# A decoder trunk on one core: K and Q blocks by seven products, a delta rule with fewer VectorE operations, and joint turns in the MLP

## The chip, the cores and the metric

The kernel runs on one core of a Trainium2 chip. The metric is the device time of one execution in microseconds (us). The engines are named as in the profile: PE (matmuls, and PEld for its weight loads), DVE (VectorE), ACT (ScalarE), POOL (GpSimd) and SP (SyncE, which here only issues DMAs). Each engine runs its own instructions in order; they wait for one another through semaphores.

## What is computed

One layer of a hybrid decoder trunk for 256 tokens of width 2048, in float32. Cut to what matters here:

```
h = rmsnorm(x)
q, k, v, z, b, a, p_in, g_a, g_b = split(h @ w_in)
q, k, v = silu(causal_dwconv(q | k | v))               # width 4
o   = gated_delta_rule(l2norm(q) * 128**-0.5, l2norm(k), v, g_log, beta)   # 16 heads of 128
y_a = rmsnorm(o) * silu(z)
y_b = einsum(pooled(p_in), pool_w) * pool_scale        # four groups of 512
x  += (sigmoid(g_a) * y_a + sigmoid(g_b) * y_b) @ w_out
gate, up = split(rmsnorm(x) @ w_up)                    # 2 x 5632
x  += (gelu(causal_dwconv(gate) + b) * up) @ w_down
return rmsnorm(x)
```

The delta rule needs, per head and chunk of tokens, decays exp(g_i - g_j) for i >= j and the solution of a unit lower triangular system.

## The kernel before

**A weight tile.** All large products read their weights from HBM as tiles of 256 rows (a feature block) by 512 columns. Each float32 value is used as a high and a low part. A tile goes through four steps: SP starts a DMA into `raw` (4 buffers); ACT copies it into `whi` (L317, 3 buffers), which rounds it; DVE subtracts to get `wlo` (L328, 3 buffers; this is called the split below); PE does 12 matmuls of 128x512: two halves `kk` of the block, two halves `t` of the tokens, and three products (high x high L365, low x high L366, high x low L367). `srcs` lists the tiles in the order in which they are used, and `weights()` returns the next one after it has started cast and split up to two tiles ahead. With three buffers the cast of tile n waits until PE has left tile n-3.

**Groups.** The input projection runs in four groups of four heads. Group g reads, eight tiles each, K, Q, V, the pooled input, the gate GB, then Z and the pool product, and the gate GA. A result is two PSUM banks, [128, 2, 512], from the pool `psm` (2 buffers); small results use `psg` (4 buffers).

**Side work.** The delta rule of group g is the generator `gdn()`, advanced by one step after each half tile (`side()`), so that its instructions lie between the matmuls of its group and of the next. It makes decays (L879 on DVE, L888 on ACT), Gram matrices (`ga`), inverts the triangular matrix's diagonal blocks of 32x32 on DVE (`B0` = 32; L965 and L967, into `tb`, which holds eight columns of a block in a partition), sends them through DRAM (`tbd`) to `TT`, and doubles the size of the inverse in steps on PE: L1011, L1029, L1039, L1047, L1054 with results taken by ACT (`U`) or DVE (L987, L1022, L1031, L1032, L1048). What is left is drained behind GA; `gated` (L1211, L1215) multiplies by the gate and adds the pooled part. Around it L1204 and L1206 apply GA and the norm weight to `sz`. Callables in `later` run behind the first tile of the next result.

**Order.** Within each engine the order comes from a scheduler which simulates a timeline over the program as it is written; from the end of group four on PE's order is fixed as written. `issue_after` adds an order between two instructions.

**Seven products.** In the MLP, pairs of feature blocks of the up projection are multiplied as 2x2 blocks (tokens in halves by features in halves, times features in halves by gate and up) with seven block products instead of eight, called T1, 11, T2, 21, T3, 22, T4. T1 to T4 use sums of weight blocks that DVE forms in `quad` tiles (L244, 128x1024), and token sums (`ups`) formed once; L1433 and similar sum partial results in PSUM. A product is 6 matmuls of 128x512 (L1418): it takes half the tokens of a tile. The results of gate and up are turned from token rows to feature rows by eight PE transposes each (L1480).

## Time and profile before

| | |
|---|---|
| three runs | 1536.61, 1536.89, 1537.75 us, median 1536.89 |
| profiled execution | span 1536.8 us |
| SP, weights of the input projection | 224 DMAs of 512 KB, 4.3 us from issue to landing |
| ACT casts of `raw`, L317 | 420, mean 1052 ns |
| DVE weight sums, L244 | 72, mean 1216 ns |

The profiled execution has no time of its own beside its span of 1536.8 us, and it is held against the median of the runs. A row of a group reads: line, engine, operation, what is written <- what is read, shape, count | busy us, mean ns | idle time of the engine just before, and what ended it. A row of a timeline reads: start, duration, engine, line, operation, in brackets the idle time before it and its releaser. Matmul records overlap, so their pitch is read from start to start. In the slices each digit is a fortieth of the span. A row of waits gives the engine, what it waited for, us in total, times and the longest.

### The profile page before, as it was taken

To read this page: it belongs to the slowest core of one execution; us is meant where nothing else is said; L and a number is where in the kernel's file an instruction comes from. 1 tells how busy PE (TensorE), PEld (TensorE's weight loads), DVE (VectorE), ACT (ScalarE), POOL (GpSimd) and SP (SyncE) were. 2 spreads that over 40 slices of the span, in tenths; PEclk is the share of its full clock that TensorE was granted. 3 is DMA by queue.
4 is the path that set the end of the run, shared out by engine and by line. 5 is a ranking of instruction groups with operands and counts; after the bars stand their busy time and mean duration, and the time that the engine had idled before them with its cause. 6 is when DMAs were issued, how large, how long until landed. Compare 5 with 4: busy or idle time off the path is not lost. (4 is left out here: it accounts for less than half of the span.)

```text
span 1536.8 us, 20233 instructions
## 1 busy us (share of the span) xinstructions
PE 1524.3 (99%) x7290; PEld 1255.4 (82%) x7290; DVE 1268.3 (83%) x1793; ACT 853.1 (56%) x1070; POOL 80.9 (5%) x105
## 2 busy tenths in 40 slices
PE   9999999999999999999999999999999999999997
PEld 8887888787878888788888888788888888888876
DVE  6788859896589858887567899999999886889896
ACT  6455446454455445454455666666666665555553
POOL 1010002000100000000000000000000011010200
PEclk9999999999999999999999999999999999999999
DMA  8776757776576766776588556656457478566662
GB/s 276 209 229 198 203 165 207 218 216 185 148 250 201 208 169 194 231 195 186 171 263 305 179 178 219 219 206 206 154 165 243 127 238 266 172 223 207 235 201 98
DMA packets 166515, 313.62 MB, mean 204 GB/s; under 512 B 19554, under 2 KB 23426, under 8 KB 166286
## 3 DMA queue, kind: packets, MB, share of 16 engines
q1 hardware_dynamic: 157280, 283.17, 59.2%
q0 software_dynamic: 7344, 27.27, 5.5%
q10 hardware_dynamic: 1790, 1.89, 0.4%
q8 instruction: 57, 0.93, 0.3%
q14 instruction: 44, 0.36, 0.1%
HBM read 303.33 MB, written 8.95 MB: 203 GB/s over the span
## 5 line engine op out<-in xcount | busy, mean ns | idle before, releaser
L317 ACT CAST whi<-raw 128x1024 fp32r<-128x1024 f32 x420 | 441.2, 1052 | 427.1 <-PE psm L366 270.0
L328 DVE TENSOR_TENSOR wlo<-raw,whi 128x1024 fp32r<-128x1024 f32 x418 | 507.7, 1220 | 146.0 <-ACT whi L317 140.2
L317 ACT CAST whi<-quad 128x1024 fp32r<-128x1024 f32 x182 | 190.5, 1053 | 136.8 <-PE psg L1418 43.5
L328 DVE TENSOR_TENSOR wlo<-quad,whi 128x1024 fp32r<-128x1024 f32 x182 | 220.0, 1219 | 30.0 <-ACT whi L317 29.4
L367 PE MATMUL psm<-wlo,xhl 128*128 128x512 f32 x432 | 169.5, 393 | 1.3 <-DVE wlo L328 1.2
L365 PE MATMUL psm<-whi,xhl 128*128 128x512 f32 x432 | 169.0, 391 | 0.0
L366 PE MATMUL psm<-whi,xhl 128*128 128x512 f32 x432 | 168.6, 390 | 0.0
L1418 PE MATMUL psg<-whi,fhl 128*128 128x512 f32 x504 | 127.2, 390 | 0.0
L1418 PEld LDWEIGHTS psg<-whi,fhl 128*128 128x128 f32 x504 | 94.5, 188 | 19.6
L367 PEld LDWEIGHTS psm<-wlo,xhl 128*128 128x128 f32 x432 | 81.1, 188 | 18.8 <-DVE wlo L328 2.2
L366 PEld LDWEIGHTS psm<-whi,xhl 128*128 128x128 f32 x432 | 81.1, 188 | 16.8
L365 PEld LDWEIGHTS psm<-whi,xhl 128*128 128x128 f32 x432 | 81.1, 188 | 16.7
L244 DVE TENSOR_TENSOR quad<-quad,quad 128x1024 f32<-128x1024 f32 x72 | 87.6, 1216 | 0.0
L1418 PE MATMUL psg<-wlo,fhl 128*128 128x512 f32 x252 | 69.9, 389 | 0.0
L1418 PE MATMUL psg<-whi,ups 128*128 128x512 f32 x216 | 58.9, 394 | 0.0
L1418 PEld LDWEIGHTS psg<-wlo,fhl 128*128 128x128 f32 x252 | 47.3, 188 | 9.9
L1403 PE MATMUL psm<-whi,hhi 128*128 128x512 f32 (+1 forms) x140 | 54.5, 389 | 0.1
L1403 PE MATMUL psm<-whi,hlo 128*128 128x512 f32 (+1 forms) x140 | 54.1, 386 | 0.0
L1403 PE MATMUL psm<-wlo,hhi 128*128 128x512 f32 (+1 forms) x140 | 54.0, 387 | 0.0
L365 PE MATMUL psm<-whi,mhi 128*128 128x512 f32 x128 | 50.8, 397 | 0.0
L367 PE MATMUL psm<-wlo,mhi 128*128 128x512 f32 x128 | 50.0, 390 | 0.0
L366 PE MATMUL psm<-whi,mlo 128*128 128x512 f32 x128 | 49.9, 390 | 0.0
(435 smaller groups left out, 2953.7 us busy)
## 6 DMA issues: line engine op xcount, KB each, us to landing
raw<-in_w_in_dram SPq DMA_DIRECT2D x224, 512.0 KB, 4.3
raw<-in_w_up_dram SPq DMA_DIRECT2D x104, 512.0 KB, 4.8
quad<-in_w_up_dram SPq DMA_DIRECT2D x72, 512.0 KB, 5.0
raw<-in_w_down_dram SPq DMA_DIRECT2D x56, 512.0 KB, 5.1
raw<-in_w_out_dram SPq DMA_DIRECT2D x32, 512.0 KB, 4.2
quad<-in_w_down_dram POOLq DMA_DIRECT2D x32, 512.0 KB, 5.3
mv<-vrow SPq DMA_DIRECT2D x12, 512.0 KB, 4.8
taps<-in_conv_qkv_w_dram SPq DMA_DIRECT2D x16, 256.0 KB, 6.6
```

The source lines that it names most:

```text
L244: nc.vector.tensor_tensor(out_, plus_, minus_, op=ALU.subtract)
L317: last_cast[0] = nc.scalar.copy(hi, raw).ins
L328: last_split[0] = nc.vector.tensor_tensor(lo, raw, hi.bitcast(F32), op=ALU.subtract).ins
L365: mm(ps[:, t, :], lh(k, t), hi[:, kk, :], start=(k == 0), stop=False)
L366: mm(ps[:, t, :], ll(k, t), hi[:, kk, :], start=False, stop=False)
L367: mm(ps[:, t, :], lh(k, t), lo[:, kk, :], start=False, stop=(k == nk - 1))
L1403: mm(ps[:, cs], lhs(kk), part_[:, kk, cs], start=(first and kk == 0 and n == 0), stop=(last and kk == 1 and n == 2), skip_group_check=shared)
L1418: mm(ps, lhs(kk), w[n][:, kk], start=(first and n == 0 and kk == 0 and lhs is high), stop=False, skip_group_check=True)
```

## The change

Three parts are changed at once.

1. In groups two to four, the first four feature blocks (tiles 0 and 1 of 256 rows) of K and of Q are computed together as a pair with seven products. K and Q play the parts of gate and up in the MLP. T1 and 11 stand between the last tiles of the GA gate of the group before (`KQ_FIRST`), the others between K's tiles (`KQ_THEN`); Q begins with its tile 2. DVE forms T1 to T4 (L266 in the changed kernel) and two PSUM sums (L406 and L415), ACT makes two copies. The token sums `xsums` are made once, in group one. Four tiles are loaded into `quad` buffers instead of `raw`.
2. In the delta rule the differences of running sums are not formed on DVE: POOL sets the excluded entries of the row to -1e30 and ACT takes exp with the negative sum as bias, one head and half at a time. The second half of `ga0` is scaled on ACT. The columns of a block are dealt to the partitions in turn, so that step j of the inversion works on only the first j // 4 + 1 of a partition's eight columns; `tb` and `tbd` are laid out for that. `gated` of groups one to three scales on ACT and uses two 128x1024 operations on DVE.
3. In the MLP, the gate and up results of a chunk are turned together behind the third pair of products instead of apart.

Lines of the changed kernel differ: L365 to L367 are now L390 to L392, L328 is L350, L244 is L266, L987 is L1039, L1011 to L1054 are L1063 to L1106, L1204 and L1206 are L1301 and L1303, L1418 is L423, L1480 is L1568.

```diff
+    UP_PARTS = ("T1", "11", "T2", "21", "T3", "22", "T4")
+    KQ_FIRST = (5, "11", 6, "T1", 7)
+    KQ_THEN = ("T2", "21", "T3", 2, "22", 3, "T4", 4, 5, 6, 7)
+    up_w = {("kq", g): [cols(w_in[0], base + 512 * g, KD) for base in (C_K, C_Q)] for g in range(1, 4)}
...
+            if g and base == C_K:
+                srcs += [("up", ("kq", g), step, 0) if isinstance(step, str) else tiles[step] for step in KQ_THEN]
+            else:
+                srcs += tiles[2:] if g and base == C_Q else tiles
...
+        srcs += tiles[: 5 if g < 3 else 8]
+        if g < 3:
+            srcs += [("up", ("kq", g + 1), step, 0) if isinstance(step, str) else tiles[step] for step in KQ_FIRST]
...
-            up_steps += p21 + [("gate", c)] + t3 + p22 + [("up", c)] + t4
+            up_steps += p21 + t3 + p22 + [("turns", c)] + t4
...
+    quads_behind = {}
+    for g in range(1, 4):
+        sums_behind[first_part(("kq", g)) - 1] = [(("kq", g), "T1", 0)]
+        for i in range(4):
+            quads_behind[first_part(("kq", g), "11") - 6 + i] = [(("kq", g), i)]
...
+    def pair_product(bank, what, tokens, sums):
+        a, b = bank["ps"]
+        if what in ("11", "21", "T4"):
+            j, t = {"11": (0, 0), "21": (1, 0), "T4": (1, 1)}[what]
+            high, low = (lambda kk, f=f: f(2 * j + kk, t) for f in tokens)
+        else:
+            n = {"T1": 0, "T2": 1, "T3": 2, "22": 3}[what]
+            high, low = (lambda kk, s=s: s[:, n, kk * P : (kk + 1) * P] for s in sums)
+        if what == "21":
+            nc.vector.tensor_tensor(b[:, 0], a[:, 1], bank["own"], op=ALU.add)
+        w = weights()
+        ps = {"T1": a[:, 0], "21": a[:, 0], "22": b and b[:, 0]}.get(what, a[:, 1])
+        high_first([(ps, high, low)], w, what in ("T1", "11"))
+        if what == "T1":
+            bank["own"] = cpool.tile([P, 512], F32, tag="sqj", name=nm("own"))
+            nc.scalar.copy(bank["own"], a[:, 0])
+            nc.scalar.copy(a[:, 0], a[:, 1])
+        elif what == "T3":
+            nc.vector.tensor_tensor(b[:, 1], a[:, 1], bank["own"], op=ALU.add)
...
-                                pattern=[[-1, 8], [1, B0]], compare_op=ALU.is_equal, fill=0.0, base=-8 * cq,
+                                pattern=[[-4, 8], [1, B0]], compare_op=ALU.is_equal, fill=0.0, base=-cq,
...
-        nc.vector.tensor_copy(cumc, pcc)
+        nc.vector.tensor_scalar(ncum, pcc, -1.0, None, op0=ALU.mult)
...
-        def differences(hp):
-            for h in (2 * hp, 2 * hp + 1):
-                for t in range(2):
-                    nc.vector.tensor_scalar(crow[:, h, t, :], crow[:, h, t, :],
-                                            cumc[:, t, 4 * g + h : 4 * g + h + 1], 0.0,
-                                            op0=ALU.subtract, op1=ALU.min)
-        differences(0)
+        def later_rows(hp):
+            d = crow[:, 2 * hp : 2 * hp + 2].rearrange("p h t i -> p (h t) i")
+            nc.gpsimd.affine_select(d, d, pattern=[[0, 4], [1, P]], compare_op=ALU.is_ge, fill=NEVER, base=0,
+                                    channel_multiplier=-1)
+        later_rows(0)
         yield
         for hp in range(2):
-            hs = slice(2 * hp, 2 * hp + 2)
-            for t, dec in ((0, dec0), (1, dec1)):
-                nc.scalar.activation(dec[:, hs, :], crow[:, hs, t, :], AF.Exp)
-            for d in (dec0[:, hs, :], dec1[:, hs, :]):
-                nc.gpsimd.affine_select(d, d, pattern=[[0, 2], [1, P]], compare_op=ALU.is_ge, fill=0.0, base=0,
-                                        channel_multiplier=-1)
+            for h in (2 * hp, 2 * hp + 1):
+                for t, dec in ((0, dec0), (1, dec1)):
+                    nc.scalar.activation(dec[:, h, :], crow[:, h, t, :], AF.Exp,
+                                         bias=ncum[:, t, 4 * g + h : 4 * g + h + 1])
             if hp == 0:
-                differences(1)
+                later_rows(1)
...
+            nc.vector.tensor_tensor(st[:, hs], sj[:, 0, hs], tail[:, 4 * g + h0 : 4 * g + h0 + 2], op=ALU.mult)
...
-                nc.vector.tensor_scalar(ga0h[:, :, next_half], pg0h[:, :, next_half], sj[:, 0, h : h + 1],
-                                        tail[:, hh : hh + 1], op0=ALU.mult, op1=ALU.mult)
+                nc.scalar.activation(ga0h[:, :, next_half], pg0h[:, :, next_half], AF.Copy, scale=st[:, h : h + 1])
...
-            tv = tmp[:, :, j + 1 :]
-            nc.vector.tensor_tensor(tv, lb[:, j, j + 1 :].unsqueeze(1).to_broadcast([P, 8, B0 - 1 - j]),
-                                    tb[:, :, j : j + 1].to_broadcast([P, 8, B0 - 1 - j]), op=ALU.mult)
-            nc.vector.tensor_tensor(tb[:, :, j + 1 :], tb[:, :, j + 1 :], tv, op=ALU.subtract)
+            n = j // 4 + 1
+            tv = tmp[:, :n, j + 1 :]
+            nc.vector.tensor_tensor(tv, lb[:, j, j + 1 :].unsqueeze(1).to_broadcast([P, n, B0 - 1 - j]),
+                                    tb[:, :n, j : j + 1].to_broadcast([P, n, B0 - 1 - j]), op=ALU.mult)
+            nc.vector.tensor_tensor(tb[:, :n, j + 1 :], tb[:, :n, j + 1 :], tv, op=ALU.subtract)
...
-        tbd = dpool.tile([32, 4, 8 * B0], F32, tag="tbd", name=nm("tbd"))
+        tbd = dpool.tile([32, 8, 4, B0], F32, tag="tbd", name=nm("tbd"))
         for cq in range(4):
-            nc.sync.dma_start(tbd[:, cq], tb[32 * cq : 32 * cq + 32].rearrange("p c i -> p (c i)"))
+            nc.sync.dma_start(tbd[:, :, cq, :], tb[32 * cq : 32 * cq + 32])
         for r in range(NR):
             rs = slice(B0 * r, B0 * (r + 1))
-            nc.sync.dma_start(TTa[rs, :, rs], tbd.rearrange("(q r) a (c i) -> r (a c) q i", q=8, i=B0)[r])
+            nc.sync.dma_start(TTa[rs, :, rs], tbd.rearrange("(q r) m a i -> r (m a) q i", q=8)[r])
...
+    def kq_steps(steps, ps, flush=3):
+        for step in steps:
+            if isinstance(step, str):
+                pair_product(pair_bank, step, (xh, xl), xsums)
+            else:
+                gemm_a(xh, xl, KD, (step,), ps, flush)
...
-            ps = ps_k0 if kind == 1 and g == 0 else gemm_a(xh, xl, KD)
+            if g == 0:
+                ps = ps_k0 if kind else gemm_a(xh, xl, KD)
+            elif kind:
+                pair_bank["ps"] = ps, b = pair_bank["ps"][0], pm()
+                kq_steps(KQ_THEN, ps)
+            else:
+                ps = gemm_a(xh, xl, KD, range(2, 8), pair_bank["ps"][1], 3)
...
-            ps = gemm_a(xh, xl, KD)
+            ps = gemm_a(xh, xl, KD, range(5))
+            pair_bank["ps"] = pm(), None
+            kq_steps(KQ_FIRST, ps, 1)
...
-        def gated(sz=sz, res=res, yb=yb):
-            po, ro = res[0]
-            for t in range(2):
-                nc.vector.tensor_tensor(sz[:, t, :], po[t].rearrange("p h d -> p (h d)"), sz[:, t, :], op=ALU.mult)
+        def gated(sz=sz, res=res, yb=yb, g=g):
+            po, ro, vt = res[0]
+            if g == 3:
+                for t in range(2):
+                    nc.vector.tensor_tensor(sz[:, t, :], po[t].rearrange("p h d -> p (h d)"), sz[:, t, :], op=ALU.mult)
+                for t in range(2):
+                    for h in range(4):
+                        hs = slice(h * P, (h + 1) * P)
+                        nc.vector.scalar_tensor_tensor(sz[:, t, hs], sz[:, t, hs], ro[:, t, h : h + 1], yb[:, t, hs],
+                                                       op0=ALU.mult, op1=ALU.add)
+                return
             for t in range(2):
                 for h in range(4):
-                    hs = slice(h * P, (h + 1) * P)
-                    nc.vector.scalar_tensor_tensor(sz[:, t, hs], sz[:, t, hs], ro[:, t, h : h + 1], yb[:, t, hs],
-                                                   op0=ALU.mult, op1=ALU.add)
+                    nc.scalar.activation(vt[:, t, h, :], po[t][:, h, :], AF.Copy, scale=ro[:, t, h : h + 1])
+            nc.vector.tensor_tensor(sz, sz, vt.rearrange("p t h d -> p t (h d)"), op=ALU.mult)
+            nc.vector.tensor_tensor(sz, sz, yb, op=ALU.add)
...
-        elif step[0] == "gate":
-            gates = turned_pair(pending[step[1], 0])
-        elif step[0] == "up":
-            ups = turned_pair(pending[step[1], 1])
+        elif step[0] == "turns":
+            gates, ups = (turned_pair(pending[step[1], col]) for col in range(2))
```

PE at the boundary from the second to the third group, before; tiles of K with the solve's products between them (`psm` is K's result, the number behind `whi` names the tile, `xhl` the tokens' high and low parts, `T` and `U` blocks of the solve):

```order
L365 MATMUL psm_1939<-whi_1974,xhl1b 128x512
L1029 MATMUL psg_1663<-U_1629,TT 32x32 x8
L1029 MATMUL psg_1676<-U_1641,TT 32x32 x8
L366 MATMUL psm_1939<-whi_1974,xhl1b 128x512
...
L365 MATMUL psm_1939<-whi_2010,xhl2b 128x512
L1039 MATMUL psg_1695<-T,ga_118_805 64x64 x2
L1039 MATMUL psg_1695<-T,ga_119_806 64x64 x2
```

Between these two steps lay the rest of tile 1974, all of 1992 and the start of 2010. After, at the same place, from product T2 to tile 2 of K (`xs` are the token sums):

```order
L1081 MATMUL psg_1693<-U_1656,TT 32x32 x8
L423 MATMUL psm_1886<-whi_1935,xs_772 128x512
...
L423 MATMUL psm_1886<-wlo_1937,xs_772 128x512 x2
L1091 MATMUL psg_1712<-T,ga_122_817 64x64 x2
...
L423 MATMUL psm_1886<-whi_1950,xhl_114 128x512 x4
L423 MATMUL psm_1886<-wlo_1952,xhl_114 128x512 x2
L423 MATMUL psm_1886<-whi_1985,xs_772 128x512
...
L1099 MATMUL psg_1742<-TT,U_1717 64x64 x4
L423 MATMUL psm_1886<-wlo_1987,xs_772 128x512 x2
L1099 MATMUL psg_1748<-TT,U_1724 64x64 x4
L1106 MATMUL psg_1762<-vt_738,TT 128x128 x2
L390 MATMUL psm_1886<-whi_1998,xhl1a 128x512
```

The solve's steps moved together: one product of 6 matmuls, or two, lies between them instead of two tiles.

DVE at the same boundary, before, from the transposes behind the blocks' way through DRAM on:

```order
L987 STREAM_TRANSPOSE T<-TT 32x8x32 x4
L328 TENSOR_TENSOR wlo_1944<-raw_1940,whi_1942 128x1024
L1204 SCALAR_TENSOR_TENSOR sz_1592<-gate_1921,sz_1592 128x1024
L328 TENSOR_TENSOR wlo_1976<-raw_1972,whi_1974 128x1024
L1206 TENSOR_TENSOR sz_1592<-sz_1592,gwb 128x1024
L1022 TENSOR_SCALAR ro_1646<-psg_1644 32x8 x4
```

Splits and the gate's two operations took turns here, one split for each tile. After, the later part of the same stretch:

```order
L266 TENSOR_TENSOR quad_1617<-quad_1774,quad_1617 128x1024
L1301 SCALAR_TENSOR_TENSOR sz_1605<-gate_1966,sz_1605 128x1024
L406 TENSOR_TENSOR psm_1984<-psm_1886,own_1947 128x512
L1084 STREAM_TRANSPOSE TT<-T 32x2x2x32 x3
L350 TENSOR_TENSOR wlo_1987<-quad_1672,whi_1985 128x1024
L1084 STREAM_TRANSPOSE TT<-T 32x2x2x32
L350 TENSOR_TENSOR wlo_2000<-raw_1996,whi_1998 128x1024
L1303 TENSOR_TENSOR sz_1605<-sz_1605,gwb 128x1024
L350 TENSOR_TENSOR wlo_2010<-quad_1734,whi_2008 128x1024
L1100 TENSOR_SCALAR TT<-psg_1742 64x2x2x64
L415 TENSOR_TENSOR psm_1984<-psm_1886,own_1947 128x512
```

L406 and L415, the two PSUM sums that PE's products 21 and tile 2 need, now stand behind the T4 sum and the gate's operations L1301 and L1303.

PE in the MLP, before: the turn of a chunk's gate results (`e`) behind the second pair of products, the turn of its up results 15 rows later behind the third (`fhl` are tokens, `ups` token sums):

```order
L1418 MATMUL psg_7582<-wlo_7645,fhl_6778 128x512 x2
L1480 MATMUL psm_7684<-ident,e_7459 128x128 x8
L1418 MATMUL psg_7515<-whi_7664,ups_7393 128x512
...
L1418 MATMUL psg_7662<-wlo_7709,ups 128x512 x2
L1480 MATMUL psm_7749<-ident,e_7659 128x128 x8
L1418 MATMUL psg_7515<-whi_7721,fhl1b 128x512 x4
```

And after:

```order
L423 MATMUL psg_7723<-whi_7759,ups 128x512 x4
L423 MATMUL psg_7723<-wlo_7761,ups 128x512 x2
L1568 MATMUL psm_7801<-ident,e_7520 128x128 x8
L1568 MATMUL psm_7810<-ident,e_7720 128x128 x8
L423 MATMUL psg_7576<-whi_7773,fhl1b 128x512 x4
```

Both turns now stand together behind the third pair of products.

More of the change, by code (lines that the diff above doesn't have):

```diff
@@ L32 @@
 LATE = (26, 24, 22, 18)
+NEVER = -1e30
 @with_exitstack
@@ L332, in begin @@
             made.append((hi, lo))
+            for more in quads_behind.get(len(made) - 1, ()):
+                quad_load(*more)
             for more in sums_behind.get(len(made) - 1, ()):
@@ L711 @@
     crd = dpool.tile([4, 4 * S], F32, tag="crd", bufs=1, name="crd")
-    cumc = mp.tile([P, 2, NH], F32, name="cumc")
+    ncum = mp.tile([P, 2, NH], F32, name="ncum")
     tail = mp.tile([P, NH], F32, name="tail")
@@ L1410, in fl @@
         return both(fhl, k)[:, 1, t * P : (t + 1) * P]
-    def high_first(uses, w, first=False):
-        for n in range(2):
-            for kk in range(2):
-                for ps, high, low in uses:
-                    for lhs in (high, low) if n == 0 else (high,):
-                        mm(ps, lhs(kk), w[n][:, kk], start=(first and n == 0 and kk == 0 and lhs is high), stop=False,
-                           skip_group_check=True)
     def up_product(c, what, ch):
@@ L1579 @@
         for n, step in enumerate(steps[hf]):
-            if hf == 0 and n == 1:
-                for _ in gate_part(NUP - 1, turned(pending[NUP - 1, 0])):
-                    pass
-            if hf == 0 and n == 2:
-                up_part(NUP - 1, turned(pending[NUP - 1, 1]))
+            if hf == 0 and n == 2:
+                gates, ups = (turned(pending[NUP - 1, col]) for col in range(2))
+                for _ in gate_part(NUP - 1, gates):
+                    pass
+                up_part(NUP - 1, ups)
             w = weights()
```

68 lines of the change are left out of this document (48 added, 20 removed).

## The prediction

> **What bounds the kernel now.** I read the page's busy times and slices first, then the chain of waits on TensorE, then single stretches of the timeline. Rows of the page:
>
> ```profile
> PE 1524.3 (99%) x7290; PEld 1255.4 (82%) x7290; DVE 1268.3 (83%) x1793; ACT 853.1 (56%) x1070; POOL 80.9 (5%) x105
> DVE  6788859896589858887567899999999886889896
> PEclk9999999999999999999999999999999999999999
> L328 DVE TENSOR_TENSOR wlo<-raw,whi 128x1024 fp32r<-128x1024 f32 x418 | 507.7, 1220 | 146.0 <-ACT whi L317 140.2
> L367 PE MATMUL psm<-wlo,xhl 128*128 128x512 f32 x432 | 169.5, 393 | 1.3 <-DVE wlo L328 1.2
> ```
>
> PE is busy 99% of a span of 1536.8 us at full clock, so the time is PE's instruction stream plus its few stalls. DVE is at 83% on average, and at 90% or more in most slices of the MLP. What PE waited for in all (total us, times, longest):
>
> ```profile
> PE psm L367 <- DVE wlo L328: 1.5, 2, 1.2
> PE psg L1418 <- DVE wlo L328: 1.2, 3, 0.8
> ```
>
> So before this change DVE costs PE 2.7 us in all. Two things can move the time: the number of matmuls, and DVE falling further behind. The span stands for the median of the runs, 1536.89 us; the sum is made against 1536.8.
>
> **Fewer matmuls: -4.1 us.** Each of three pairs needs seven products of 6 matmuls (42) where four plain tiles took 4 x 12 = 48, so 18 matmuls of 128x512 go. Their pitch, and the stretch in which the pair will stand, in PE's timeline at the first boundary of groups (K of group two):
>
> ```profile
> 181.73 0.39 PE L367 MATMUL psm<-wlo,xhl 128*128 128x512 f32 x1
> 188.53 0.39 PE L367 MATMUL psm<-wlo,xhl 128*128 128x512 f32 x1
> ...
> 211.98 0.40 PE L365 MATMUL psm<-whi,xhl 128*128 128x512 f32 x1
> 212.22 0.61 PE L1054 MATMUL psg<-vt,TT 128*128 128x128 f32 x4
> ...
> 213.12 0.39 PE L365 MATMUL psm<-whi,xhl 128*128 128x512 f32 x1
> ```
>
> Thirty matmuls lie between the first two rows: 6.80 / 30 = 0.2267 us, and 18 x 0.2267 = 4.08 us. The L1054 products push the last row from 0.68 (three pitches) to 1.14, so they cost 0.46. The other solve products (L1011, L1029, L1039, L1047) stand between 188.53 and 211.98:
>
> ```profile
> 188.70:212.00 23.30, 23.30 (x181) 18.75 (x181) 14.89 (x25) 9.46 (x14) 0.00 (x0) 1.00 0.64 180
> ```
>
> PE's first pair of numbers: 181 instructions, 98 of them small ones of the solve and 83 large. Large ones take 82 x 0.2267 = 18.59 of the 23.45 us, the solve 4.86. PE has no stall here, and DVE (third pair) is busy 14.89 of 23.30 us, because the solve's steps lie 18 to 28 matmuls apart.
>
> **The pair's price on DVE: +14.7 us.** Seven products instead of four tiles need three more splits, four 128x1024 weight sums and two 128x512 sums in PSUM. In the new order of PE, between the start of product "11" and the start of tile 2 of K stand 54 large matmuls (12.24 us) and now all the solve steps (4.86 + 0.46), so PE has 17.6 us of work there. DVE's queue from behind the split of tile 6 up to the second PSUM sum (L415), for which tile 2's first matmul waits, is in the new order: four sums, seven splits, L1301 and L1303 (the gate's 128x1024 operations) make 13 operations of 128x1024; beside them stand the solve's own steps and the two PSUM sums. Their durations, from DVE's timeline at the same boundary and in the MLP:
>
> ```profile
> 178.66 0.18 DVE L967 TENSOR_TENSOR tb<-tb,tmp 128x8 f32<-128x8 f32 x1
> 182.34 1.23 DVE L328 TENSOR_TENSOR wlo<-raw,whi 128x1024 fp32r<-128x1024 f32 x1 [1.49 <-ACT whi L317]
> 185.82 1.84 DVE L987 STREAM_TRANSPOSE T<-TT 32x256 f32<-32x256 f32 x4 [2.25 <-DMA TT<-tbd]
> 187.69 1.23 DVE L328 TENSOR_TENSOR wlo<-raw,whi 128x1024 fp32r<-128x1024 f32 x1
> 188.83 1.22 DVE L1204 SCALAR_TENSOR_TENSOR sz<-gate,sz 128x1024 f32<-128x1024 f32 x1
> 189.97 1.22 DVE L328 TENSOR_TENSOR wlo<-raw,whi 128x1024 fp32r<-128x1024 f32 x1
> ...
> 192.24 0.68 DVE L1022 TENSOR_SCALAR ro<-psg 32x8 f32<-32x8 f32 x4
> 192.95 1.23 DVE L328 TENSOR_TENSOR wlo<-raw,whi 128x1024 fp32r<-128x1024 f32 x1
> 195.90 1.26 DVE L1031 TENSOR_SCALAR T<-psg 32x128 f32<-32x128 f32 x4
> 197.18 1.31 DVE L1032 STREAM_TRANSPOSE TT<-T 32x128 f32<-32x128 f32 x4
> 198.52 1.23 DVE L328 TENSOR_TENSOR wlo<-raw,whi 128x1024 fp32r<-128x1024 f32 x1
> 207.41 0.42 DVE L1048 TENSOR_SCALAR TT<-psg 64x256 f32<-64x256 f32 x1 [1.24 <-PE psg L1047]
> 207.75 1.21 DVE L328 TENSOR_TENSOR wlo<-raw,whi 128x1024 fp32r<-128x1024 f32 x1
> ```
>
> ```profile
> 1088.37 0.69 DVE L1433 TENSOR_TENSOR psg<-psg,own 128x512 f32<-128x512 f32 x1
> 1088.97 1.22 DVE L328 TENSOR_TENSOR wlo<-quad,whi 128x1024 fp32r<-128x1024 f32 x1
> ```
>
> Start to start, a 128x1024 operation takes 1.14 (187.69 to 188.83 to 189.97), L987 1.87, L1022 0.71, L1031 1.28, L1032 1.34, L1048 0.34 and a PSUM sum 0.60. The queue is 13 x 1.14 + 1.87 + 0.71 + 1.28 + 1.34 + 0.34 + 2 x 0.60 = 21.6 us of work without a gap. It can't be begun much ahead, since a cast waits for PE to leave the tile three earlier:
>
> ```profile
> 181.25 1.05 ACT L317 CAST whi<-raw 128x1024 fp32r<-128x1024 f32 x1 [1.67 <-PE psm L366]
> ```
>
> The split starts 1.09 after its cast (182.34) and frees DVE 1.14 later. Tile 6's cast can start when PE reaches tile 5, one tile (2.72 us) before "11", so DVE is through with its split at -0.5 us, counted from "11". L415 then ends at 21.1 at the earliest, against 17.6 us of PE work: at least 3.5 us of stall at a boundary. Nothing behind it covers this, for PE has no other work in its order.
>
> The likelier size is larger. L1039 (before: L987) waits for the transposed blocks that go through DRAM: from tb's last operation (ends 178.84) to L987 (185.82) 7.0 us pass, and in the third group the same chain took 6.2:
>
> ```profile
> 535.43 0.18 DVE L967 TENSOR_TENSOR tb<-tb,tmp 128x8 f32<-128x8 f32 x1
> 541.63 1.37 DVE L987 STREAM_TRANSPOSE T<-TT 32x256 f32<-32x256 f32 x3 [1.75 <-DMA TT<-tbd]
> ```
>
> In the new order tb's last operation follows the split of tile 5, at about -5.6 (three tiles of cover, 8.2, less 1.09, 1.14 and two small operations), so the blocks land at +1.4, while DVE would reach L1039 at 0.6. That is 0.8 us, and I add 0.6 for DVE at the solve's PSUM results, which PE gives only between its own matmuls. 21.1 + 1.4 = 22.5, a stall of 4.9 per boundary, and 3 x 4.9 = 14.7. The ends: 3.5 each (10.5) if the blocks land early, and 6.0 each (18.0) if the rewritten transfer, which now goes in shorter runs, is 1.1 us later. I expect the waits ahead of "21" (about 1.6 us, for L406 behind the T4 sum and L1301) and at L1106 and tile 2 (2.2 to 2.8, for L1100 and L415 behind L1303 and two splits). The four loads for the weight sums go out on SP behind the raw tiles of the gate's first blocks and replace four raw loads there, so that SP's queue is no longer than before; they cost nothing while they land before the T1 sum. The two PSUM copies (ACT) lie under the 12 matmuls of tile 7.
>
> **Less work in the delta rule: -1.2 us.** What goes from DVE, by forms:
>
> ```profile
> L879 DVE TENSOR_SCALAR crow<-crow,cumc 128x128 f32<-128x128 f32 x32 | 7.4, 292 | 8.1 <-DMA crow<-crd 8.1
> L923 DVE TENSOR_SCALAR ga<-psg,sj,tail 128x256 f32<-128x256 f32 x16 | 8.5, 532 | 0.0
> L1215 DVE SCALAR_TENSOR_TENSOR sz<-sz,ro,yb 128x128 f32<-128x128 f32 x32 | 9.3, 360 | 0.0
> ```
>
> L879 is 1.9 us a group and L923 2.1. The block inversion handles 1560 of 3968 elements per partition; at about 1 ns each in two operations that is 4.8 us a group. In `gated` of three groups eight L1215 (2.9) and two 128x512 products (1.4) become two operations of 1.14, 2.0 less. About 11 us of DVE a group, but DVE time counts only where PE waits, which outside the MLP is 1.5 us in two places. The larger is this one, in the third group:
>
> ```profile
> 452.43 1.23 DVE L816 TENSOR_TENSOR mv<-mv,taps 128x1024 f32<-128x1024 f32 x1 [4.48 <-DMA mv<-vrow]
> ...
> 460.95 0.50 PE L367 MATMUL psm<-wlo,xhl 128*128 128x512 f32 x1 [1.20 <-DVE wlo L328]
> ```
>
> It comes from a DMA at the head of DVE's queue (splits stood behind it), not from DVE's load, so I take half of it, the other 0.3 whole, and 0.3 for delays too short for that view. [...] The ends are 0 and -2.7. ACT gains 8 scalings of 0.4 us in one piece in `gated`, about 3.1 us; a cast is started 5.4 us ahead of its tile and needs 2.2 with its split, so 3.2 us of cover just hold, and if they don't it is +1.
>
> **Joint turns in the MLP: -0.7 us.** Before, the turn of the gate's results (8 transposes) stands alone:
>
> ```profile
> 1090.03 1.04 PE L1480 MATMUL psm<-ident,e 128*128 128x128 f32 x8
> 1090.82 1.17 PE L1418 MATMUL psg<-whi,ups 128*128 128x512 f32 x4
> ```
>
> The large matmuls keep their count. One break in PE's stream instead of two saves at most 0.13 us (two breaks with four products, 0.46 each as at 212.22, against 0.79 for eight transposes in one) and at least nothing; I take a fifth, 0.3 in eleven chunks, since transposes run on without a gap either way. DVE's taps move behind the splits of the third products, which may take 0.4 of the 1.2 us of L1418's waits, or, with cover lost, add up to 0.2 a chunk: ends -2.6 and +2.2.
>
> **Sum.** 1536.8 - 4.1 + 14.7 - 1.2 - 0.7 = 1545.5 us.
>
> **Rivals.** *Faster: DVE's backlog never forms.* If DVE gets through its queue 3.5 us and more earlier, because it has gaps of 2.25 and 1.49 us in the rows above, the pair's matmuls are pure gain: 1536.8 - 4.1 - 1.2 - 0.7 = 1530.8. Those gaps were waits for a cast and a DMA that stay where they are, which speaks against it; it decides if L415 ends before 17.6.
> *The floor:* blocks early and no waits at PSUM, 10.5 instead of 14.7: 1541.3, and with the full reliefs 1539.
> *Longer, with the clock.* Three waits of 6.0 give 1548.8. PEclk is 9 all along, and the longest hole in PE's rows was 1.2 us, so the trace doesn't show what a longer one does. [...] My holes are nearer to the 1.2 us that left the clock alone than to twice that much again, so it gets a small part of this rival's chance. [...]
>
> **How the numbers follow.** Forecast 0.52 (its own range 1541 to 1549); floor 0.17, a third of it below 1540; faster 0.13; longer 0.18, most of it under 1552. The predicted time is 1545.5. The range 1536 to 1551.5 leaves out the faster case and the clock. A measurement here tells 0.2% (3.1 us) from no change: faster 0.13, same 0.08 (the low end of the floor and a half-hidden queue), slower 0.79.
>
> **What would show it.** In the new profile PE should wait for L406, L1100 and L415 at three boundaries, some 5 us each, with DVE without gaps from split 6 on; DVE's share falls in the group stage elsewhere; PE has 18 fewer large matmuls and a PEclk of 9. If PE shows no such waits, the queue argument is wrong; if waits appear at K's or Q's later tiles or in the MLP instead, the terms are misplaced.

## The result and the profile after

| | before | after |
|---|---|---|
| runs beside each other | 1536.61 to 1537.75 us, median 1536.78 | 1548.24 to 1555.53 us, median 1549.98 |
| profiled execution | span 1536.8 us | 1548.99 us, span 1547.3 us |

The change makes the kernel slower: the ratio of after to before is 1.0089, interval [1.0075, 1.0102]. A second series, `e11_after_again` below, gave 1.0079 [1.0066, 1.0091]. In the four runs of the changed kernel the time is 1.7 us above the span.

The page of the changed kernel, the rows that answer to those shown of before:

```profile
PE 1525.7 (99%) x7272; PEld 1256.4 (81%) x7272; DVE 1265.8 (82%) x1763; ACT 881.9 (57%) x1142; POOL 74.1 (5%) x97
PEclk9999999999999999999999999999999999999999
L392 PE MATMUL psm<-wlo,xhl 128*128 128x512 f32 x384 | 150.7, 392 | 0.2 <-DVE wlo L350 0.2
```

PE has 18 instructions fewer, is still "busy 99%", and every slice of PEclk reads 9. DVE works 2.5 us less than before, and K's, Q's and the other plain tiles wait 0.2 us for DVE (last row) instead of 1.2. None of these rows names a loss. Only the difference of span and busy time does: PE is idle for 21.6 us (1547.3 - 1525.7) where it was idle for 12.5, and it is busy 1.4 us longer although 18 matmuls went. The loss stands in three places too short for a slice of 38.7 us. PE's waits find them:

```profile
PE psm L423 <- DVE psm L406: 7.5, 3, 2.7
PE psg L423 <- DVE psg L1521: 2.6, 4, 0.7
PE psg L1106 <- DVE TT L1100: 1.4, 3, 0.5
```

Three waits for L406, three for L1100: the three boundaries of groups. The row between them lies in the MLP and is taken up further below. PE's timeline at the first boundary, from product "11" (first row) to tile 2 of K (last row):

```profile
178.24 1.07 PE L423 MATMUL psm<-whi,xhl 128*128 128x512 f32 x4
...
193.62 1.23 PE L423 MATMUL psm<-whi,xhl 128*128 128x512 f32 x4 [2.36 <-DVE psm L406]
...
195.51 1.91 PE L423 MATMUL psm<-whi,xs 128*128 128x512 f32 x4
...
200.07 0.71 PE L1106 MATMUL psg<-vt,TT 128*128 128x128 f32 x4 [0.47 <-DVE TT L1100]
200.68 0.50 PE L390 MATMUL psm<-whi,xhl1a 128*128 128x512 f32 x1
```

From the first row to the last 22.4 us pass; the other boundaries take 22.5 and 22.8. With the prediction's 17.56 us of PE work there, the stalls are 4.9, 5.0 and 5.2 us, 15.0 in all. PE's listed waits account for 2.8, 2.9 and 3.1 us of them. Most of the rest lies around 195.51: four matmuls in 1.91 us, 0.46 us from start to start, twice the usual 0.2267. The granted clock in four stretches of this boundary (the number behind POOL's pair):

```profile
190.00:193.00 3.00, 1.26 (x17) 1.00 (x16) 2.91 (x5) 1.81 (x4) 0.00 (x0) 1.00 0.00 0
193.00:195.00 2.00, 1.38 (x5) 1.19 (x6) 1.88 (x5) 0.11 (x1) 0.00 (x0) 0.91 0.00 0
195.00:198.00 3.00, 3.00 (x12) 1.97 (x11) 2.94 (x4) 1.49 (x2) 0.00 (x0) 0.50 0.00 0
198.00:200.00 2.00, 1.60 (x15) 1.03 (x13) 2.00 (x4) 0.50 (x1) 0.00 (x0) 0.99 0.73 183
```

About 1 us after PE resumed, its clock fell to half for 3.4 us, which is 1.7 us of its work. A slice of the page averages that away. Here it cost nothing extra, because tile 2 waited for DVE's queue in any case, as DVE's own timeline shows (from the split of tile 6 to the second PSUM sum):

```profile
176.58 1.23 DVE L350 TENSOR_TENSOR wlo<-raw,whi 128x1024 fp32r<-128x1024 f32 x1 [1.50 <-ACT whi L339]
177.72 1.22 DVE L266 TENSOR_TENSOR quad<-quad,quad 128x1024 f32<-128x1024 f32 x1
178.86 1.95 DVE L1039 STREAM_TRANSPOSE T<-TT 32x256 f32<-32x256 f32 x4
...
185.67 1.23 DVE L350 TENSOR_TENSOR wlo<-quad,whi 128x1024 fp32r<-128x1024 f32 x1 [0.73 <-ACT whi L339]
...
190.48 1.23 DVE L266 TENSOR_TENSOR quad<-quad,quad 128x1024 f32<-128x1024 f32 x1
191.62 1.22 DVE L1301 SCALAR_TENSOR_TENSOR sz<-gate,sz 128x1024 f32<-128x1024 f32 x1
192.87 0.70 DVE L406 TENSOR_TENSOR psm<-psm,own 128x512 f32<-128x512 f32 x1
...
197.34 1.22 DVE L1303 TENSOR_TENSOR sz<-sz,gwb 128x1024 f32<-128x1024 f32 x1
198.47 1.22 DVE L350 TENSOR_TENSOR wlo<-quad,whi 128x1024 fp32r<-128x1024 f32 x1
199.61 0.41 DVE L1100 TENSOR_SCALAR TT<-psg 64x256 f32<-64x256 f32 x1
199.94 0.68 DVE L415 TENSOR_TENSOR psm<-psm,own 128x512 f32<-128x512 f32 x1
```

From 177.72 to the end of L415 at 200.62 DVE works 22.9 us with a single gap, 0.73. PE runs out of work while DVE does operations that PE does not need yet: the T4 sum (190.48) and L1301 (191.62) stand ahead of L406; L1303 and the split of product 22 (198.47) ahead of L415.

Where the 10.5 us between the two spans lie: by the start of the same matmuls, the changed trace is behind by 3.3 us at V of group two, 6.3 at V of group three, 9.2 at V of group four, 9.2 at the start of the MLP and 11.1 at its end.

### The profile page after: what moved, and what is told of

It is laid out like the page before. It is cut to its first block, busy times and chain, and to the rows that moved or that the text cites. A ratio compares the mean times of both kernels' runs of the same rounds, so it can differ in the third digit from the quotient of the medians.

```text
span 1547.3 us, 20200 instructions
## 1 busy us (share of the span) xinstructions
PE 1525.7 (99%) x7272; PEld 1256.4 (81%) x7272; DVE 1265.8 (82%) x1763; ACT 881.9 (57%) x1142; POOL 74.1 (5%) x97
## 4 chain that ended last, share of the span: by engine, by line
PE 90%; DVE 6%; DMA 2%; issue 1%; ACT 1%; SPq 0%; POOL 0%; POOLq 0%; DVEq 0%; ACTq 0%
PE psg L423 26%; PE psm L390 13%; PE psm L392 13%; PE psm L391 13%; PE psm L1500 7%; PE psg L1500 7%; DVE wlo L350 3%; PE psm L423 2%; PE psm L566 1%; PE psm L1568 1%; DVE quad L266 1%; PE psg L465 1%; PE psg L953 1%; DMA raw<-in_w_in_dram 1%; ACT whi L339 1%
## 5 line engine op out<-in xcount | busy, mean ns | idle before, releaser
L339 ACT CAST whi<-raw 128x1024 fp32r<-128x1024 f32 x408 | 428.3, 1052 | 371.5 <-PE psm L391 204.7
L350 DVE TENSOR_TENSOR wlo<-raw,whi 128x1024 fp32r<-128x1024 f32 x406 | 495.8, 1225 | 143.2 <-ACT whi L339 135.0
L339 ACT CAST whi<-quad 128x1024 fp32r<-128x1024 f32 x203 | 212.6, 1053 | 179.8 <-DVE quad L266 42.8
L350 DVE TENSOR_TENSOR wlo<-quad,whi 128x1024 fp32r<-128x1024 f32 x203 | 246.8, 1224 | 40.4 <-ACT whi L339 38.7
L392 PE MATMUL psm<-wlo,xhl 128*128 128x512 f32 x384 | 150.7, 392 | 0.2 <-DVE wlo L350 0.2
L390 PE MATMUL psm<-whi,xhl 128*128 128x512 f32 x384 | 150.2, 391 | 0.0
L391 PE MATMUL psm<-whi,xhl 128*128 128x512 f32 x384 | 149.5, 389 | 0.0
L423 PE MATMUL psg<-whi,fhl 128*128 128x512 f32 x504 | 127.1, 389 | 0.0
L423 PEld LDWEIGHTS psg<-whi,fhl 128*128 128x128 f32 x504 | 94.5, 188 | 19.5
L266 DVE TENSOR_TENSOR quad<-quad,quad 128x1024 f32<-128x1024 f32 x84 | 102.6, 1222 | 0.1
L392 PEld LDWEIGHTS psm<-wlo,xhl 128*128 128x128 f32 x384 | 72.1, 188 | 15.9 <-DVE wlo L350 1.0
L391 PEld LDWEIGHTS psm<-whi,xhl 128*128 128x128 f32 x384 | 72.1, 188 | 14.8
L390 PEld LDWEIGHTS psm<-whi,xhl 128*128 128x128 f32 x384 | 72.1, 188 | 14.6
L423 PE MATMUL psg<-wlo,fhl 128*128 128x512 f32 x252 | 69.8, 389 | 0.0
L423 PE MATMUL psg<-whi,ups 128*128 128x512 f32 x216 | 58.2, 391 | 2.6 <-DVE psg L1521 2.6
L423 PEld LDWEIGHTS psg<-wlo,fhl 128*128 128x128 f32 x252 | 47.3, 188 | 9.8
L390 PE MATMUL psm<-whi,mhi 128*128 128x512 f32 x128 | 50.8, 397 | 0.0
L423 PEld LDWEIGHTS psg<-whi,ups 128*128 128x128 f32 x216 | 40.2, 188 | 12.4 <-DVE psg L1521 2.3
L392 PE MATMUL psm<-wlo,mhi 128*128 128x512 f32 x128 | 49.9, 390 | 0.0
```

What stands on the lines that cost most here:

```text
L266: nc.vector.tensor_tensor(out_, plus_, minus_, op=ALU.subtract)
L339: last_cast[0] = nc.scalar.copy(hi, raw).ins
L350: last_split[0] = nc.vector.tensor_tensor(lo, raw, hi.bitcast(F32), op=ALU.subtract).ins
L390: mm(ps[:, t, :], lh(k, t), hi[:, kk, :], start=(k == 0), stop=False, **seeded)
L391: mm(ps[:, t, :], ll(k, t), hi[:, kk, :], start=False, stop=False, **seeded)
L392: mm(ps[:, t, :], lh(k, t), lo[:, kk, :], start=False, stop=(k == nk - 1), **seeded)
```

## The experiments

The theory under test is the prediction's: between "11" and tile 2, DVE has about 22.5 us in its queue and PE 17.6, and PE waits out the difference. Rivals: another part of the change carries the loss; the place of the products in PE's order does; the drop of the clock does. Times are medians; each ratio is to the kernel before, run beside it on the same chip (medians 1537.94, 1538.07 and 1537.98 for the three groups of runs).

### Which part carries it

`e1_no_pair`: K and Q computed plainly, as before; the delta rule and the joint turns stay changed.

```diff
...
-            elif kind:
-                pair_bank["ps"] = ps, b = pair_bank["ps"][0], pm()
-                kq_steps(KQ_THEN, ps)
...
+            ps = ps_k0 if kind == 1 and g == 0 else gemm_a(xh, xl, KD)
...
```

> The changed kernel without the pair: K and Q of groups two to four as eight plain tiles each, the delta rule and the joint turns as changed. Theory (the pair's queue on DVE is the loss): the three boundaries give back 15.1 us of stalls and take 4.1 us of matmuls, so the time falls by about 11 us from the changed kernel's profiled execution and ends at 1536 to 1537 us, with the granted clock back at 0.998. Rival (a good part of the loss lies in the delta rule or the turns): the time stays above 1541 us.

Measured: 1536.56 us, 0.9992 [0.9983, 1.0002], ten runs, as the theory had it. No wait for L406 or L1100 is left.

`e6_delta_only`: the kernel before with the delta rule's part alone.

```diff
...
-            up_steps += p21 + t3 + p22 + [("turns", c)] + t4
+            up_steps += p21 + [("gate", c)] + t3 + p22 + [("up", c)] + t4
...
```

(beside the edit of e1, the turns go back)

> The kernel before with the delta rule's part of the change alone (no pair, turns apart). Theory (DVE relief counts where PE waited for splits): the trace after has 1.95 us less up to the fourth group outside the pairs, so 1.5 to 2 us faster than before. Rival (moving work to ACT costs what it gives): within 0.5 us of before.

Measured: 1536.95 us, 0.9991 [0.9982, 0.9999]: a gain of 1.1 us by the medians, less than the 1.5 to 2 us expected.

`e7_turns_only`: the kernel before with the joint turns alone (the diff above, reversed, in the kernel before).

> The kernel before with the joint turns alone. The prediction gave them -0.7 us. Theory after the trace (the PSUM sum now queues behind the gate's taps on DVE): PE waits for that sum 1.5 to 2.6 us and the MLP is 1 to 2 us longer. Rival (as predicted): 0.3 to 0.7 us faster.

Measured: 1537.61 us, 1.0000 [0.9991, 1.0009]: not told from no change. Neither the theory (1 to 2 us longer) nor its rival came true, though PE waited 1.5 us for that sum.

`e2_pair_apart`: the changed kernel with the turns apart again.

> The changed kernel with the turns of gate and up apart, as before; pair and delta rule as changed. The prediction gave the joint turns -0.7 us, and the trace after shows 2.6 us of new waits of PE for the PSUM sum behind the taps against 1.2 us of old ones. Theory (joint turns cost about 1.5 us by those waits): 1.5 us faster than the changed kernel, and no waits of PE on that sum. Rival (joint turns gain or are neutral): equal, or up to 0.7 us slower.

Measured: 1548.73 us, 1.0078 [1.0060, 1.0095], where the changed kernel has 1.0089 and 1.0079. The gain of 1.5 us that was expected can't be told here. The pair carries the loss: with it the ratio is 1.008 to 1.009, without it 0.999 to 1.000.

### Taking work out of the queue

`e3_sz_late`: L1301 and L1303 are ordered behind L415, so two operations of 1.14 us leave the queue; `gated`, which needs them, moves behind them.

```diff
...
-        nc.vector.scalar_tensor_tensor(sz, ta, 1.0, sz, op0=ALU.add, op1=ALU.mult)
...
+        def both_gates(sz=sz, ta=ta, g=g):
+            behind = ExitStack()
+            if g < 3:
+                behind.enter_context(tc.issue_after(pair_bank["t3"]))
+            nc.vector.scalar_tensor_tensor(sz, ta, 1.0, sz, op0=ALU.add, op1=ALU.mult)
...
             drain()
-            gated()
+            later.append(both_gates)
+            later.append(gated)
```

> The changed kernel with the GA gate's two 128x1024 operations on DVE ordered behind the second PSUM sum of the pair; nothing else changed. Theory (DVE's queue decides when tile 2 begins): the queue is 2.3 us shorter, the start of product 11 to the start of tile 2 takes 20.2 us instead of 22.5, and three boundaries give 6.9 us: 1542 to 1543 us by the median. Rival one (the blocks' way through DRAM or the solve's own chain decides): no change. Rival two (the halved clock after the wait is what costs): the wait for the first PSUM sum falls from 2.4 to about 1.3 us, the clock stays at full, and the gain is 6.9 plus up to 1.7 us a boundary.

Measured: 1542.19 us, 1.0029 [1.0017, 1.0041]. From "11" to tile 2: 20.2, 20.3 and 21.0 us, so 2.3, 2.2 and 1.7 less for 2.28 taken out; the time is what the theory had (1542 to 1543). PE's waits for L406, two rows of PE's timeline at the first boundary, and its stretch of 7 us (the clock is the 1.00 behind POOL's pair):

```profile
PE psm L423 <- DVE psm L406: 4.2, 3, 1.6
```

```profile
192.12 1.20 PE L423 MATMUL psm<-whi,xhl 128*128 128x512 f32 x4 [1.23 <-DVE psm L406]
...
197.42 0.71 PE L1106 MATMUL psg<-vt,TT 128*128 128x128 f32 x4 [0.86 <-DVE TT L1100]
```

```profile
190.00:197.00 7.00, 5.33 (x44) 3.92 (x41) 6.75 (x11) 3.53 (x5) 0.00 (x0) 1.00 0.01 2
```

The wait for L406 went from 2.36 to 1.23 (L1301 gone from ahead of it), and the clock stayed at 1.00. At the third boundary it did not: the wait there was 1.58 us, the clock was at half from 550.04 to 553.45, and this time the drop cost something. DVE's L415 waited 0.20 us for PE, and PE reached tile 2 without another wait, 0.7 us later than at the second boundary.

`e9_tuned`: beside L1301 and L1303, the T4 sum and the split of product 22 are ordered behind L415: four operations, 4.56 us.

```diff
...
-        w = weights()
+        w = weights(1 if what == "T3" else AHEAD)
...
-            nc.vector.tensor_tensor(b[:, 1], a[:, 1], bank["own"], op=ALU.add)
+            bank["t3"] = nc.vector.tensor_tensor(b[:, 1], a[:, 1], bank["own"], op=ALU.add).ins
+            last_conv["pair"] = bank["t3"]
+            with tc.issue_after(bank["t3"]):
+                up_sum(bank["c"], "T4", 0)
```

> The changed kernel with four operations of 128x1024 moved behind the second PSUM sum in DVE's queue at each boundary: the gate's two, the T4 sum (its product comes four steps later) and the split of product 22. Theory (DVE's queue against PE's work): the queue from tile 6's split to the second PSUM sum is 21.6 - 4 x 1.14 = 17.0 us, PE's work 17.6, so the stall falls from 5 us to under 1 us a boundary; by the run with the gate's operations late (stalls of 2.6 to 3.4 us, 4 us above the kernel before) 6 to 7 us are left to win, which makes 2 to 3 us less than the kernel before. The granted clock returns to 0.998 in all runs. Rival (the solve's own chain, or ACT, takes over as in the spread pair): a stall of 2 us or more remains and the time stays above the kernel before.

Measured: 1533.81 us, 0.9970 [0.9958, 0.9982]: faster than before. From "11" to tile 2: 18.1, 18.0 and 18.2 us. PE's waits at the first PSUM sum (at two of the three boundaries), DVE's timeline at the first boundary, and PE's busy time there (first pair):

```profile
PE psm L430 <- DVE psm L408: 0.6, 2, 0.4
```

```profile
191.18 0.70 DVE L408 TENSOR_TENSOR psm<-psm,own 128x512 f32<-128x512 f32 x1
...
195.98 0.68 DVE L417 TENSOR_TENSOR psm<-psm,own 128x512 f32<-128x512 f32 x1
196.58 1.21 DVE L268 TENSOR_TENSOR quad<-quad,quad 128x1024 f32<-128x1024 f32 x1
197.71 1.21 DVE L352 TENSOR_TENSOR wlo<-quad,whi 128x1024 fp32r<-128x1024 f32 x1
...
199.98 1.21 DVE L1313 SCALAR_TENSOR_TENSOR sz<-gate,sz 128x1024 f32<-128x1024 f32 x1
```

```profile
190.00:200.00 10.00, 9.75 (x65) 7.50 (x64) 9.69 (x17) 4.68 (x7) 0.00 (x0) 1.00 0.19 54
```

The two PSUM sums (here L408 and L417) come first, the T4 sum, the split and the gate behind them. DVE is as busy as in the changed kernel (9.69 of 10 us, third pair, against 9.72 in the four stretches shown above); only the order in its queue differs. The stall is 1.7 us in three boundaries instead of 15.0.

`e10_tuned_apart`: the same with the turns apart.

> The same with the turns of gate and up apart. Theory (the turns are worth less than can be measured, as alone on the kernel before): within 1 us of the run beside it. Rival (in a kernel with DVE nearer to its limit the joint turns cost 1 us or more): 1 us or more faster.

Measured: 1532.70 us, 0.9968 [0.9956, 0.9980]: 1.1 us less than e9 by the medians, not told apart from it.

`e11_after_again`: the changed kernel beside e9 and e10.

> The changed kernel once more, on the chip of these runs. Theory: 11 to 13 us above the kernel before, with times that spread over several us, and the longer the lower the granted clock of the run, since a wait of 2.4 us ahead of the first PSUM sum lets the clock drop and the drop lasts differently from run to run. Rival (the clock has nothing to do with the spread): time and granted clock don't go together.

Measured: 1550.16 us, 1.0079 [1.0066, 1.0091]; boundaries 22.4, 22.4 and 22.8 us. Against e9 on the same chip that is 16.4 us, of which the stalls make 13.3.

### Giving PE more time instead

`e4_spread`: the products stand farther apart, so that more of PE's own tiles lie between "11" and tile 2.

```diff
-    KQ_FIRST = (5, "11", 6, "T1", 7)
-    KQ_THEN = ("T2", "21", "T3", 2, "22", 3, "T4", 4, 5, 6, 7)
+    KQ_FIRST = (3, "11", 4, "T1", 5, "T2", 6, 7)
+    KQ_THEN = ("21", "T3", 2, "22", 3, "T4", 4, 5, 6, 7)
```

> The changed kernel with the pair spread out: product 11 behind tile 3 of GA, then tile 4, T1, tile 5, T2, tiles 6 and 7, and the rest as before. Theory (DVE's queue against PE's work): from 11 to tile 2 PE has 24 more matmuls (5.4 us) and DVE two more splits (2.3 us), so the stall falls from 4.9 to about 1.8 us a boundary, 9 us in three: 1540 to 1541 us. Rival (a fixed wait for something that ends late, such as the gate's result or the blocks): the stall stays near 5 us and the time near 1549 us.

Measured: 1544.78 us, 1.0046 [1.0029, 1.0063]; 5 to 7 us better than the change, where the theory had 9. The timelines of PE, ACT and DVE at the first boundary:

```profile
193.16 1.14 PE L1099 MATMUL psg<-TT,U 64*64 64x64 f32 x16 [1.52 <-ACT U L1093]
196.41 2.07 PE L423 MATMUL psm<-whi,xhl 128*128 128x512 f32 x4 [2.11 <-DVE psm L406]
```

```profile
191.45 1.27 ACT L1272 ACTIVATE gate<-psm,rsh 128x512 f32<-128x512 f32 x2
192.74 0.64 ACT L1093 COPY U<-psg 64x256 f32<-64x256 f32 x2
```

```profile
194.41 1.22 DVE L1301 SCALAR_TENSOR_TENSOR sz<-gate,sz 128x1024 f32<-128x1024 f32 x1
195.66 0.70 DVE L406 TENSOR_TENSOR psm<-psm,own 128x512 f32<-128x512 f32 x1
```

"21" now follows the gate's last tile directly, but L406 stands behind L1301, which needs the gate's result, and the copy of `U` stands behind the gate (1.27) on ACT. More work for PE ahead of these does not help: they can start only when GA is done. These two waits stand at the first boundary alone, and the clock was at half there for 6.8 us, from within the second of them on. From "11" to V of the next group the trace loses 6.9 us net against the kernel before at this boundary, 2.1 at the second, where the clock stayed at 1.00, and 4.0 at the third, where it was at half for 3.4 us. So in this kernel the drop of the clock is a rival for part of the loss; no run takes the two apart.

`e5_best`: spread, e3's edit and turns apart together. `e8_best2`: the same with the products farther apart still.

```diff
+    KQ_FIRST = (2, "11", 3, 4, "T1", 5, 6, "T2", 7)
+    KQ_THEN = ("21", "T3", 2, "22", 3, 4, "T4", 5, 6, 7)
```

> Pair spread out as in the run with that name, the gate's two DVE operations behind the second PSUM sum, turns apart, delta rule as changed. Theory (DVE's queue and what stands ahead of the first PSUM sum in it): PE has 23.5 us of work or more from product 11 to tile 2, DVE's queue 21.6 + 2.3 - 2.3 = 21.6, so only the sum's own wait behind tile 2's split is left (tile 7 leaves PE, 1.05 of cast, 1.14 of split, 0.6 of sum against 2.6 of solve products), under 1 us a boundary. The pair then keeps at least 1 us of its 4.1, and with the delta rule's 2 us the kernel is 2 to 4 us faster than the one before. Rival (the pair costs what DVE and ACT do for it wherever it stands): no faster than before.

> As the spread pair with late gate operations and turns apart, but spread further: 11 behind tile 2 of GA, tiles 3 and 4, T1, tiles 5 and 6, T2, tile 7, and K's tile 4 ahead of T4. Theory: no DVE queue is left at all, so it equals the run beside it within 1 us, both bounded by the wait for the first PSUM sum behind tile 2's split. Rival (density still decides): 2 us or more faster than the run beside it.

Measured: 1542.07 us, 1.0028 [1.0017, 1.0039], and 1541.84 us, 1.0025 [1.0015, 1.0035]. The expectation for e5 missed, and its rival (no faster than before) held. e8 came within 0.3 us of e5, as its theory had it, but not for its reason: its trace has no wait for L406. PE's waits of e5:

```profile
PE psm L392 <- DVE wlo L350: 4.0, 5, 1.5
PE psg L1099 <- ACT U L1093: 1.5, 1, 1.5
```

At the first boundary PE waits for the copy of `U` (1.5) and for L406 (1.0), which stands behind the split of tile 2. The two longest waits for L350 (1.5 and 1.4) lie far from the boundaries. The clock fell to half at the first boundary alone, in both kernels, and from "11" to V this boundary lost 4.8 us in e5 and 4.0 in e8, the other two 1.3 to 1.7 each. What makes up these losses stays open. The next edit went back to the changed kernel's places and moved work within DVE's queue.

### The sums on another engine

`e12_pool_sums`: the pair's weight sums run on POOL, which is idle there (0.00 us busy from 178.23 to 200.66 in the changed kernel).

```diff
+            if isinstance(c, tuple):
+                nc.gpsimd.tensor_tensor(out_, plus_, minus_, op=ALU.subtract)
+                continue
```

> The changed kernel with the pair's four weight sums on POOL instead of DVE. Theory (DVE's queue): DVE has 4.6 us less to do ahead of the second PSUM sum, so the stall of 5 us a boundary falls to about 1 us if POOL makes a sum in under 2 us, and the time to about 1539 us. Rival (POOL is slow at 128x1024, 3 us or more a sum, and PE waits for the splits of T1 to T3 behind it): the stall stays at 5 us or grows, and the wait is named at the splits of the sums.

Measured: 1553.25 us, 1.0105 [1.0090, 1.0120]. The rival held for the time: from "11" to tile 2 it takes 25.0, 24.5 and 22.0 us, longer than in the changed kernel at two of three boundaries; at these two the clock was at half for 6.8 and 3.4 us, at the third not at all. Its sign did not show: PE's longest waits are for the first PSUM sum (5.1 us in three), not for the splits of the sums. The group of the sums, a cast that waits for one, and the split behind that cast:

```profile
L266 POOL TENSOR_TENSOR quad<-quad,quad 128x1024 f32<-128x1024 f32 x12 | 33.5, 2789 | 198.8 <-DMA quad<-in_w_in_dram 82.4 <-DVE wlo L353 68.7 <-ACT whi L342 43.9
```

```profile
187.33 2.00 ACT L342 CAST whi<-quad 128x1024 fp32r<-128x1024 f32 x2 [2.00 <-POOL quad L266]
```

```profile
188.41 2.43 DVE L353 TENSOR_TENSOR wlo<-quad,whi 128x1024 fp32r<-128x1024 f32 x1 [2.78 <-ACT whi L342]
```

A sum takes 2.79 us on POOL against 1.22 on DVE, so the chain of sum, cast and split got longer, and DVE idled 2.78 us for it. The split then took 2.43 us instead of 1.23, with POOL's sum running beside it until 189.77; what stretched it this run does not show.

## Why the prediction was right, and where it was off

- **Fewer matmuls, -4.1.** The page has 7272 instead of 7290. With the stalls nearly gone, the sum of the first two terms and the delta rule's 1.7 is -4.1 + 1.7 - 1.7 = -4.1; e9 measured 1537.98 - 1533.81 = 4.2 below before. The faster rival's condition (L415 ending before PE needs it) is what e9 comes near to, by another order in the queue.
- **The pair's price, +14.7.** Measured 15.0. The step held in size and place, and e3 and e9 show its cause: 2.28 us out of the queue gave 2.1 per boundary, 4.56 gave 4.4. Its composition was partly wrong: the wait for the blocks through DRAM did not come (L1039 follows at 178.86 without a gap), a wait for a cast of 0.73 came instead, and the small operations took more than their rows of before.
- **Where PE waits.** At L406 2.4 to 2.7 us, where about 1.6 was forecast; at L1106 0.5 instead of 2.2 to 2.8 with tile 2. The sum is the same, because half clock in between (1.7 us of work) used up the time that would have been waited. The page shows it as busy time: 4.1 us of matmuls went and 5.1 us of half clock came.
- **The delta rule, -1.2.** Alone it gave 1.1 us (e6). In the changed trace 1.7 lie outside the boundaries (10.9 net of the pair against 9.2 at the MLP's start); PE's waits for the splits of plain tiles fell from 1.5 to 0.2. In e6 they are gone, also the one of 1.20 behind the DMA, of which the sum took half; DVE waited 2.25 us for that DMA there instead of 4.48. In e5, with the same part, DVE waited 3.46 and PE 1.52 behind it, so that relief does not hold in every kernel with this part. The 1 ns that the prediction takes for an element of the inversion is what the trace of before has: the operations of L965 go from 176 ns at 128x8 to 417 at 128x248.
- **Joint turns, -0.7.** Mis-sized: alone 1.0000 [0.9991, 1.0009]. In the changed trace the MLP lost 1.9 us, with new waits for L1521 of 2.6 us in four. In e11's trace, the same kernel, they are 1.5 in two and the MLP lost 0.2. So the 1.9 belong to one execution, and the turns are worth about nothing.
- **The sum, 1545.5.** That is 8.7 above before's span. The two traces differ by 10.5: the MLP is 2.6 worse than forecast for the turns, the pair 0.3, the delta rule 0.5 better, and what follows the MLP 0.6 shorter. e11's traced execution has a span of 1545.3, 8.5 above. The medians differ by 13.2. The median of 1549.98 lies within the range, but above the forecast's own 1541 to 1549: that it is inside owes something to the room left at the upper end. The trace of before was an execution with 1.7 us more than its median (1536.8 + 1.7 against 1536.78); the changed kernel's had 1.0 less than its. The step of the prediction that failed is the one about the clock. It took holes of up to 2.8 us to be near the 1.2 that left the clock alone. Waits of 2.36 to 2.69 us were followed by half clock, and in e3 one of 1.58. The length of one hole does not tell it: in e3 a wait of 1.23 us was not followed by it, in e4 two of 0.76 and 0.67 us were. In the traced executions of the changed kernel DVE's queue hid the drop; over the runs the times go up as the mean granted clock goes down:

| kernel | time us (mean granted clock), in order |
|---|---|
| after | 1548.24 (0.996), 1548.99 (0.995), 1550.97 (0.991), 1555.53 (0.989) |
| e11, the same | 1547.00 (0.996), 1549.16 (0.995), 1549.76, 1550.55, 1550.85 and 1553.53 (0.992) |
| e9 | 1532.12 to 1534.37 (all 0.999) |

Half clock for 3.4 us at three boundaries is 5.1 us of lost clock, 0.0033 of 1547: that is what a mean of 0.995 to 0.996 holds against 0.999. The same estimate, 0.007 to 0.010 of some 1550 us, gives 11 to 16 us of lost clock for the runs with 0.992 to 0.989. In which places is open, since only one execution of a series has a trace. e11's distance from e9 exceeds the stalls' difference by 3.1 us (16.4 - 13.3), as much as e11's median lies above its traced execution (1550.16 - 1547.00); that this is the clock is argued from the table, not shown.

Two figures of the prediction do not follow from its rows; neither enters the sum. The chain through DRAM in the third group took 6.0 us by the count that gives 7.0 in the first (541.63 less the end at 535.61), not 6.2. The floor with both reliefs in full is 1541.3 - 1.5 - 1.9 = 1537.9, not 1539.

## What to carry to other kernels

When a product is traded for additions on another engine, compare at the place itself: the time that engine's in-order queue takes between two points, and the bounding engine's work between the same points. Shares of busy time do not show this (DVE is at 83% before, 82% after and 83% in e9). If the queue is longer, look for operations in it that nobody needs yet, and order them behind the results that are waited for: three such orders turned a loss of 0.8 to 0.9% into a gain of 0.3% (the delta rule's part alone gives 0.1%), while work moved to a slower engine, or products spread out, made new waits.

## What the runs showed of the hardware

- TensorE's clock fell to 0.50 for 3.41 us at each of the three boundaries of the changed kernel, from 194.65, 375.55 and 556.46 us on. The drops began 0.6 to 1.2 us after the matmuls resumed behind single waits of 2.36, 2.45 and 2.69 us; in the 3.41 us ahead of them PE was busy for 1.05, 1.17 and 0.72 us. In e4 the clock was at half for 6.8 us at the first boundary. The 3.41 us ahead of the drop in e3, and the drop itself (the clock is behind POOL's pair):

```profile
546.62:550.03 3.41, 1.82 (x20) 1.33 (x19) 3.22 (x7) 2.27 (x4) 0.00 (x0) 1.00 0.00 0
550.04:553.45 3.41, 3.41 (x9) 2.67 (x10) 3.25 (x6) 1.04 (x1) 0.00 (x0) 0.50 0.00 0
```

  Not every wait was followed by a drop: behind 1.58 us at the third boundary of e3 the clock fell, behind 1.23 at its first it stayed at 1.00. In e4 two waits of 0.76 and 0.67 us, which ended at 555.42 and 556.80, stood ahead of a drop. What decides between these cases stays open.
- A 128x1024 float32 sum of two inputs took 2.79 us on POOL (mean of 12) and 1.22 us on DVE (mean of 72), 2.3 times, in e12, where DVE was busy beside it.
